# Row sums of the spatial weights: VectorE and a trip through DRAM in place of a TensorE product with ones

## The chip, the cores and the metric

The kernel runs on one core of a Trainium2 chip. TensorE (PE in the profile, PEld for its weight loads) multiplies; VectorE (DVE), ScalarE (ACT) and GpSimd (POOL) compute beside it; SyncE (SP), ScalarE and GpSimd issue DMAs. The metric is the device time of one launch in microseconds (us), compared as a median of runs.

## The reference

Two layers of a bidirectional encoder over 512 positions and 1024 channels, in float32. Each layer normalises its input, projects it into three branches (a gated linear recurrence, a spatial gating unit, windowed attention), gates them, merges them and adds the result to its input. What the change touches is the spatial gating unit:

```python
def layer_norm(x, g, b):
    mu = jnp.mean(xf, axis=-1, keepdims=True)
    var = jnp.mean(jnp.square(xf - mu), axis=-1, keepdims=True)
    return (xf - mu) * lax.rsqrt(var + EPS) * g + b

def spatial_gating(u, v, ln_g, ln_b, w_s, b_s):
    B, L, _ = u.shape
    vn = layer_norm(v, ln_g, ln_b).reshape(B, L // SG_CHUNK, SG_CHUNK, SG_GROUPS, SG_GW)
    mixed = jnp.einsum('gts,bnsgc->bntgc', w_s, vn) + b_s.T[None, None, :, :, None]
    return u * mixed.reshape(B, L, SG_W)
```

There are 4 groups of 128 channels and chunks of 128 positions. The layer norm's bias `b` is the same at every position, so it contributes `b[c]` times the sum over s of `w_s[g, t, s]`. The kernel uses that: it mixes the normalised values without gain and bias, and adds `b[c] * sum_s w_s[g, t, s] + b_s[g, t]` afterwards. These sums, 4 x 128 numbers a layer, are what the change computes in another way.

## The kernel before

Weights come in 512 KB pieces (`wr`, four buffers, loaded through SyncE in a fixed order). Each is split into a high part by ScalarE (L267, `wh`) and a low part by VectorE (L268, `wl`), and TensorE makes three products for each pair of operands. A `t_block` (L517) is 24 such products of 128 x 512, with `main_t` as its caller for the input projection; `nat_part` (L470) does the same in the other orientation. `w_ahead` (L278) issues the split of the next piece, and the loads behind it, at the end of a block.

Around these blocks the smaller work runs as Python generators. After half a block and after its end the main line calls `advance(us)`, which adds that much credit and then steps the first two generators (`WIDTH = 2`) of the list `sides` in turn, each step giving back its cost. A generator that yields `None` is not stepped again in the same call:

```python
        try:
            c = next(g)
        except StopIteration:
            sides.remove(g)
            return 0.0
        if c is None:
            waiting.append(g)
            return 0.0
```

This sets the order of the code. The framework beneath then orders each engine's queue by that order and by when operands are expected to be ready; an instruction wrapped in `pin` stays behind the one before it on its engine. Tiles of one tag share a fixed number of buffers: `t2` (128 x 512 float32) has seven, `small` 24.

The stages around the change, in each layer: projections for attention; values of the recurrence; then, for each of four heads, four blocks, and after two heads the recurrence of that pair joins `sides` (`gla`, with L915 to L974 as its steps up the levels and L992 to L1031 as its end). Attention (`attention`, L783 to L818) is in `sides` from earlier on. At h == 1 the v path of the gating unit is projected (`do_vb`), the generator `ln_v` is put second in `sides`, and, in layer 0, the row of rotary gains and sink logits for the next layer is loaded again (`rope_row`, L336, pinned on SyncE; its one buffer is read by attention up to L792). `do_uz` (L1039 to L1101) projects u and z, with a `t2` tile for z.

`ln_v` takes the statistics of v on VectorE (L1054, L1055), a reciprocal root in small operations (L324 to L331), the sums by a product of `ones` with the transposed spatial weights `ws` (L1059), so that every partition holds all of them, and four operations that turn `br`, the spatial bias on all partitions, into the sum named above (L1062). Then it normalises v in place (L1067). `spatial` (L1073 to L1078) uses `ws`, v and `br` for each group after h == 3.

`ws` and `br` are loaded by `gate_consts` (L352, L354), unpinned, through SyncE. On GpSimd's queue stand attention's two DMAs for each block of probabilities (L817 to DRAM, L818 back), the rotations' (L692, L694), and the saving of parts of the normalised input (L1295).

Of the kernel before, what the change touches and what calls it, by code (L numbers as in the profile page):

```python
# [14 lines left out]
F32 = mybir.dt.float32  # L15
# [3 lines left out]
ALU = mybir.AluOpType  # L19
AX = mybir.AxisListType.X  # L20
PSUM = bass.MemoryType.PSUM

P = 128
# [149 lines left out]
    return bass.AP(a.tensor, a.offset + off, [list(a.ap[0])] + [list(d) for d in dims])  # L173


def hybrid_kernel(tc, x, wpk, brow, gainb, pvec, wsp, trig, amask, imask, out):
    nc = tc.nc
    from contextlib import ExitStack

    with ExitStack() as es:  # L180
        cp = es.enter_context(tc.tile_pool(name="const", bufs=1))
        wp = es.enter_context(tc.tile_pool(name="wts", bufs=4))
        sb = es.enter_context(tc.tile_pool(name="work", bufs=2))
        pp = es.enter_context(tc.tile_pool(name="psum", bufs=3, space=PSUM))
        dp = es.enter_context(tc.tile_pool(name="spill", bufs=1, space=bass.MemoryType.DRAM))
        build(nc, tc, cp, wp, sb, pp, dp, x, wpk, brow, gainb, pvec, wsp, trig, amask, imask, out)


LAG, QLAG = 8, 11
N_M4, N_T2, N_PM, N_PS = 19, 7, 3, 5  # L190


def build(nc, tc, cp, wp, sb, pp, dp, x, wpk, brow, gainb, pvec, wsp, trig, amask, imask, out):
    V, S, G, E = nc.vector, nc.scalar, nc.gpsimd, nc.tensor


# [2 lines left out]
    def nm(s):  # L199
        cnt[0] += 1  # L200
        return f"{s}_{cnt[0]}"
# [7 lines left out]
    def small(n):  # L209
        return sb.tile([P, n], F32, name=nm("sm"), tag="small", bufs=24)  # L210
# [4 lines left out]
    def ps_side(shape=(P, 512), dt=F32):  # L215
        return pp.tile(list(shape), dt, name=nm("ps"), tag="ps", bufs=N_PS)
# [94 lines left out]
    ones = cp.tile([P, P], F32, name="ones")  # L311
# [9 lines left out]
    def rstd(ss, n, scale, order=free, small=small):  # L321

        v, y, a = small(n), small(n), small(n)
        order(V.tensor_scalar(v, ss, -0.5 * scale, -0.5 * EPS, ALU.mult, ALU.add))  # L324

        magic = float(0x5F3759DF - 0x40400000)
        order(V.tensor_scalar(y.bitcast(I32), v.bitcast(I32), -0.5, magic, ALU.mult, ALU.add))
        for _ in range(3):
            order(V.tensor_tensor(a, y, y, ALU.mult))
            order(V.tensor_tensor(a, a, v, ALU.mult))  # L330
            order(V.scalar_tensor_tensor(y, a, 1.5, y, ALU.add, ALU.mult))  # L331
        return y
# [17 lines left out]
    def gate_consts(l, eng):  # L350
        br = cp.tile([P, R_GQ], F32, name=nm("br"), tag="br", bufs=1)
        eng.dma_start(br, brow[l, :R_GQ].partition_broadcast(P))  # L352
        ws = cp.tile([P, 4, P], F32, name=nm("ws"), tag="ws", bufs=1)
        eng.dma_start(ws, wsp[l])  # L354
        return br, ws
# [235 lines left out]
    for l in range(L):  # L591
# [4 lines left out]
        lnb = pvc[:, V_LNB + 4 * l : V_LNB + 4 * l + 4]  # L596
# [57 lines left out]
        def main_t():  # L654
            po = t_block(*w_next(), 0, *hT, KT, lambda: advance(2.6))
            w_ahead(1)
            return po
# [205 lines left out]
        for g in range(4):  # L863
# [6 lines left out]
            po = main_t()  # L870
# [13 lines left out]
        br, ws = gate_consts(l, nc.sync)  # L884
# [162 lines left out]
            gelu(po, vg[tb // 2][:, tb % 2, :])  # L1047

        def ln_v():
            mv = small(8)  # L1050
            mv2 = mv.rearrange("p (n c) -> p n c", c=2)
            for n in range(NT):
                st = small(6)
                V.bn_stats(st, vg[n // 2][:, n % 2, :])  # L1054
                V.bn_aggr(mv2[:, n, :], st)  # L1055
            r = rstd(mv2[:, :, 1], NT, 1.0)

            po = ps_side((P, 4, P))
            E.matmul(po, ones, ws, start=True, stop=True)  # L1059
            for g in range(4):  # L1060
                b = br[:, g * P : (g + 1) * P]
                V.scalar_tensor_tensor(b, po[:, g, :], lnb[:, g : g + 1], b, ALU.mult, ALU.add)  # L1062
            yield 2.5
            yield None
            for n in range(NT):
                v = vg[n // 2][:, n % 2, :]
                V.tensor_scalar(v, v, mv2[:, n, 0:1], r[:, n : n + 1], ALU.subtract, ALU.mult)  # L1067
                yield 0.7

        def spatial(g):  # L1070
            po = ps_side((P, 4, P))
            for n in range(NT):
                E.matmul(po[:, n, :], vg[n // 2][:, n % 2, g * P : (g + 1) * P], ws[:, g, :], start=True, stop=True)  # L1073
            y = t2((P, 4, P))
            bs = br[:, R_BS + g * P : R_BS + (g + 1) * P].unsqueeze(1).broadcast_to((P, 4, P))
            V.scalar_tensor_tensor(y, po, lng[:, g : g + 1], bs, ALU.mult, ALU.add)
            u = uz[g // 2][:, g % 2, :]
            V.tensor_tensor(u, u, y.rearrange("p n t -> p (n t)"), ALU.mult)  # L1078
            yield 2.0
# [15 lines left out]

        glas = []
        lnv, spat = ln_v(), [spatial(g) for g in range(4)]
        for h in range(H):
            po = main_t()
# [4 lines left out]
            for d in range(2):  # L1104
                po = main_t()
                gates(po, d, h, ff, kd)
                advance(2.6)
            po = main_t()
# [272 lines left out]
        def quarter(slot, half):  # L1381
            return three(lambda ts, kt, g: ts[kt][:, slot, 256 * half + g * P : 256 * half + (g + 1) * P], mgh, mgl)
# [57 lines left out]
        def one(terms, handler, *args):  # L1440
            return product(terms, 1, (P, 1, 512), lambda g, po: handler(g, po[:, 0]), *args)

        a = one(quarter(0, 0), p1)
# [15 lines left out]
def host_arrays(inputs):  # L1459
    a = {k: np.asarray(v) for k, v in inputs.items()}  # L1460
    ct = np.ascontiguousarray
    f = a["x"].dtype
    arrays = {}
    arrays["x"] = ct(a["x"].reshape(T, D))
    arrays["wpk"] = pack_weights(a["w_in"], a["w_branch_a"], a["w_branch_b"], a["w_branch_c"], a["w_out"])

    def swap(g):
        return np.concatenate([g[:, 32:], g[:, :32]], axis=1)

    qg, kg = a["q_norm_gain"], a["k_norm_gain"]  # L1470
    arrays["brow"] = ct(
        np.concatenate(
            [
                a["b_spatial"].reshape(L, 512),
                qg,
                swap(qg),
                kg,
                swap(kg),
                a["sink_logits"],
            ],  # L1480
            axis=1,
        )
    )
    arrays["gainb"] = ct(a["norm_gain"])
    lbl = a["lb_logits"].reshape(L, 8, P).transpose(2, 0, 1).reshape(P, 16)
    hgt = a["hg_norm_gain"].transpose(2, 0, 1).reshape(P, 8)
    lnt = [a[n].reshape(L, 4, P).transpose(2, 0, 1).reshape(P, 8) for n in ("sg_ln_gain", "sg_ln_bias")]
    arrays["pvec"] = ct(np.concatenate([lbl, hgt] + lnt, axis=1))
    arrays["wsp"] = ct(a["w_spatial"].transpose(0, 3, 1, 2))

    half = 32
    inv = (10000.0 ** (-np.arange(half, dtype=np.float64) / half)).astype(np.float32)
    ang = np.arange(T, dtype=np.float32)[:, None] * inv[None, :]
    c = np.cos(ang.astype(np.float64)).astype(np.float32)
    s = np.sin(ang.astype(np.float64)).astype(np.float32)
    cc = np.concatenate([c, c], axis=1).reshape(NT, P, 64).transpose(1, 0, 2)
    sn = np.concatenate([-s, s], axis=1).reshape(NT, P, 64).transpose(1, 0, 2)
    arrays["trig"] = ct(np.stack([cc, sn], axis=1))
    qi, ki = np.arange(P)[:, None], np.arange(P)[None, :]
    arrays["amask"] = ct(  # L1500
        np.concatenate(
            [np.where(ki >= qi, 0.0, MASKED), np.zeros((P, P)), np.where(ki <= qi, 0.0, MASKED)], axis=1
        ).astype(np.float32)
    )
    si, ti = (np.arange(P) % 32)[:, None], np.arange(32)[None, :]
    xr = si ^ ti
    masks = [(xr >= m) & (xr < 2 * m) for m in (1, 2, 4, 8)]
    masks += [(xr < 16) & (np.arange(P)[:, None] // 32 == b) for b in range(4)]
    arrays["imask"] = ct(np.stack(masks, axis=1).astype(np.int32))
    assert arrays["x"].dtype == f  # L1510
    return arrays


NAMES = ["x", "wpk", "brow", "gainb", "pvec", "wsp", "trig", "amask", "imask"]


# [16 lines left out]
```

## Time and profile before

| | |
|---|---|
| time, median of 3 runs | 1064.62 us (1064.45 to 1065.05) |
| the profiled execution | 1064.73 us, span 1063.0 us |
| granted TensorE clock | 1.00 |
| TensorE busy | 1054.4 us, 7432 instructions |
| VectorE busy | 799.7 us, 1497 instructions |
| ScalarE busy | 521.4 us, 797 instructions |
| GpSimd busy | 106.7 us, 150 instructions |
| DMA | 162.78 MB, mean 153 GB/s |

The span runs from the first to the last instruction; the profiled execution's own time contains it and what lies around it. A row of a line or a group names the line of the code, the engine and operation, the tile written and those read, and durations in ns (least, median, most). A timeline row gives the start in us, the duration, the engine and the line; "x2" means two instructions merged in one row, and a bracket gives the engine's idle time before it and what ended it. The ends of matmuls are modelled.

### The profile page before, as it was taken

How to read it: one execution, taken by the hardware profiler on the slowest of the kernel's cores; microseconds unless marked ns; L12 is line 12 of the kernel's file. 1: busy time of each engine (PE TensorE's matmuls, PEld its weight loads, DVE VectorE, ACT ScalarE, POOL GpSimd, SP SyncE). 2: the span in 40 equal slices, each digit the busy share in tenths (PEclk: the TensorE clock that was granted, in tenths of full speed). 3: DMA queues.
4: the chain of work that ended last, by engine and by line, in shares of the span. 5: the costliest groups of instructions: out<-in, count | busy, mean ns of one | idle time of the engine just before them, and what ended most of it. 6: DMA issues, size and time to landing. Idle time of an engine off the chain costs nothing.

```text
span 1063.0 us, 18544 instructions
## 1 busy us (share of the span) xinstructions
PE 1054.4 (99%) x7432; PEld 893.7 (84%) x7432; DVE 799.7 (75%) x1497; ACT 521.4 (49%) x797; POOL 106.7 (10%) x150
## 2 busy tenths in 40 slices
PE   8999999999999999999999999999999999999998
PEld 7888877888788998988878888777878889999886
DVE  6884699877877865578887567998678678665885
ACT  5344874464523652545433377656553245345442
POOL 0220111000000100001102201100000001010030
PEclk9999999999999999999999999999999999999999
DMA  8673464252333465665958345543432236466664
GB/s 311 165 226 101 156 199 159 102 183 82 118 120 82 101 195 120 159 221 108 304 162 239 124 137 168 179 133 120 159 107 91 102 60 159 140 142 179 201 174 137
DMA packets 49734, 162.78 MB, mean 153 GB/s; under 512 B 5744, under 2 KB 10352, under 8 KB 49648
## 3 DMA queue, kind: packets, MB, share of 16 engines
q1 hardware_dynamic: 28656, 100.25, 28.6%
q0 software_dynamic: 19264, 57.16, 21.7%
q10 hardware_dynamic: 1728, 4.20, 1.0%
q8 instruction: 58, 0.95, 0.3%
q14 instruction: 28, 0.23, 0.1%
HBM read 139.55 MB, written 22.02 MB: 152 GB/s over the span
## 4 chain that ended last, share of the span: by engine, by line
PE 95%; DVE 2%; DMA 1%; ACT 1%; issue 0%; SPq 0%; ACTq 0%; POOLq 0%; DVEq 0%
PE pm L517 49%; PE pm L470 12%; PE ps L1193 11%; PE pm L1193 11%; PE pm L505 2%; PE ps L831 2%; PE ps L926 1%; PE ps L782 1%; PE ps L781 1%; PE ps L1000 1%; PE ps L1073 1%; PE ps L1012 1%; DMA wr<-in_wpk 1%; PE ps L1016 1%; PE ps L948 1%; DMA hold<-in_wpk 1%
## 5 line engine op out<-in xcount | busy, mean ns | idle before, releaser
L267 ACT CAST wh<-wr 128x1024 fp32r<-128x1024 f32 x160 | 166.7, 1050 | 213.2 <-PE pm L517 135.8
L268 DVE TENSOR_TENSOR wl<-wr,wh 128x1024 fp32r<-128x1024 f32 x160 | 193.5, 1219 | 78.5 <-PE pm L517 32.6
L517 PE MATMUL pm<-hth,wh 128*128 128x512 f32 x576 | 229.9, 399 | 0.0
L517 PE MATMUL pm<-htl,wh 128*128 128x512 f32 x576 | 224.9, 390 | 0.0
L517 PE MATMUL pm<-hth,wl 128*128 128x512 f32 x576 | 224.6, 390 | 0.0
L517 PEld LDWEIGHTS pm<-hth,wh 128*128 128x128 f32 x576 | 108.2, 188 | 25.8 <-issue 2.9
L517 PEld LDWEIGHTS pm<-hth,wl 128*128 128x128 f32 x576 | 108.1, 188 | 22.9
L517 PEld LDWEIGHTS pm<-htl,wh 128*128 128x128 f32 x576 | 108.3, 188 | 20.9 <-issue 0.5
L517 PE MATMUL pm<-m,wh 128*128 128x512 f32 x256 | 89.8, 391 | 0.0
L470 PE MATMUL pm<-wh,hth 128*128 128x512 f32 x192 | 74.4, 397 | 0.7 <-ACT hth L267 0.5
L470 PE MATMUL pm<-wh,htl 128*128 128x512 f32 x192 | 73.5, 392 | 0.2 <-DVE htl L268 0.2
L470 PE MATMUL pm<-wl,hth 128*128 128x512 f32 x192 | 73.2, 391 | 0.0
L972 DVE TENSOR_TENSOR m<-m,f 128x512 f32<-128x512 f32 x96 | 63.2, 685 | 6.3 <-PE ps L948 5.0
L268 DVE TENSOR_TENSOR wl<-hold,wh 128x1024 fp32r<-128x1024 f32 x36 | 43.7, 1221 | 22.6 <-PE pm L1193 16.7
L267 ACT CAST wh<-hold 128x1024 fp32r<-128x1024 f32 x36 | 37.7, 1049 | 43.4 <-PE pm L517 15.6
L517 PEld LDWEIGHTS pm<-m,wh 128*128 128x128 f32 x256 | 47.8, 188 | 9.5
L517 PE MATMUL pm<-t,wl 128*128 128x512 f32 x128 | 50.2, 393 | 0.0
L517 PE MATMUL pm<-t,wh 128*128 128x512 f32 x128 | 50.0, 390 | 0.0
L470 PEld LDWEIGHTS pm<-wh,hth 128*128 128x128 f32 x192 | 36.0, 188 | 10.3 <-issue 1.6
L267 ACT CAST m<-m 128x512 fp32r<-128x512 f32 (+1 forms) x30 | 24.2, 819 | 38.2 <-DVE m L1314 22.1
L470 PEld LDWEIGHTS pm<-wh,htl 128*128 128x128 f32 x192 | 36.0, 188 | 7.7 <-DVE htl L268 0.5
L470 PEld LDWEIGHTS pm<-wl,hth 128*128 128x128 f32 x192 | 36.0, 188 | 7.4
(258 smaller groups left out, 2247.0 us busy)
## 6 DMA issues: line engine op xcount, KB each, us to landing
wr<-in_wpk SPq DMA_DIRECT2D x160, 512.0 KB, 3.9
pd<-m POOLq DMA_DIRECT2D x20, 512.0 KB, 4.0
m<-pd POOLq DMA_DIRECT2D x20, 512.0 KB, 4.8
hold<-in_wpk POOLq DMA_DIRECT2D x18, 512.0 KB, 5.5
hold<-in_wpk SPq DMA_DIRECT2D x12, 512.0 KB, 4.9
wr<-in_wpk POOLq DMA_DIRECT2D x12, 512.0 KB, 7.0
m<-in_x SPq DMA_DIRECT2D x8, 512.0 KB, 6.7
m<-xd POOLq DMA_DIRECT2D x16, 256.0 KB, 6.9
```

The source lines that it names most:

```text
L267: order(S.copy(hi_dst, src))
L268: order(eng.tensor_tensor(lo_dst, src, hi_dst.bitcast(F32), ALU.subtract))
L470: E.matmul(po, a, b[:, o : o + 512], start=first and n == 0, stop=last and n == len(passes) - 1)
L505: E.matmul(po[:, k, :], a, b[:, o : o + 256], start=n == 0, stop=n == 23)
L517: E.matmul(po, s, m, start=n == 0, stop=n == 3 * nk - 1)
L781: E.matmul(sp[:, :nk], qt[qb][:, h, :], ktt[0][:, g, k0 * P : k1 * P], start=True, stop=False)
L782: E.matmul(sp[:, :nk], qt[qb][:, h, :], ktt[1][:, g, k0 * P : k1 * P], start=False, stop=True)
L831: E.matmul(po[64 * g : 64 * g + 64], vC[:, k0 + kb, 64 * g : 64 * g + 64], pt[:, :, 128 * g : 128 * g + 128], start=kb == 0, stop=kb == le ...
L926: E.matmul(cb[p0 : p0 + 32, slot, j // 4, :], kk(32 * j), qq(32 * j), start=True, stop=True, tile_position=(0, p0),)
L948: E.matmul(dg[p0 : p0 + 32, j // 4, f0 : f0 + 32], kx[:, 32 * j : 32 * j + 32] if m == 16 else k_op(32 * j, m), q_op(32 * jq, m), start=Tr ...
L972: V.tensor_tensor(v, v, custom(ff, of, ([sd, 2], [2, ng], [0, m])), ALU.mult)
L1193: E.matmul(banks[g][:, r, :], a, b, start=not onto and (r, kt, n) == (0, 0, 0), stop=kt == 3 and n == 2, skip_group_check=onto is not None ...
```

## The change

The host hands over the spatial weights in a second layout, `wsr`, with the position t on the partitions and s innermost. `ln_v` begins with a `t2` tile `wsum`, which is loaded with them through SyncE, and then yields `None` three times. After that VectorE sums over s, which leaves one number for each t (partition) and group. GpSimd's queue writes these 128 x 4 numbers to DRAM in the order group, t, and reads them back, to every partition, into the same `wsum`. The product with ones is gone; the four operations on `br` read `wsum` in place of PSUM, and stand after the normalisation of v in place of before it. Two yields of 0.5 are added.

```diff
+    arrays["wsr"] = ct(a["w_spatial"].transpose(0, 2, 1, 3))
...
         def ln_v():
+
+            wsum = t2((P, 4, P))
+            nc.sync.dma_start(wsum, wsr[l])
+            for _ in range(3):
+                yield None
+            ss = small(4)
+            V.tensor_reduce(ss, wsum, AX, ALU.add)
+            sd = dp.tile([4, P], F32, name=nm("sd"))
+            G.dma_start(sd.rearrange("g t -> t g"), ss)
+            G.dma_start(wsum.rearrange("p g t -> p (g t)"), sd.rearrange("g t -> (g t)").partition_broadcast(P))
+            yield 0.5
             mv = small(8)
             mv2 = mv.rearrange("p (n c) -> p n c", c=2)
             for n in range(NT):
@@
                 V.bn_aggr(mv2[:, n, :], st)
             r = rstd(mv2[:, :, 1], NT, 1.0)
-
-            po = ps_side((P, 4, P))
-            E.matmul(po, ones, ws, start=True, stop=True)
-            for g in range(4):
-                b = br[:, g * P : (g + 1) * P]
-                V.scalar_tensor_tensor(b, po[:, g, :], lnb[:, g : g + 1], b, ALU.mult, ALU.add)
             yield 2.5
             yield None
             for n in range(NT):
                 v = vg[n // 2][:, n % 2, :]
                 V.tensor_scalar(v, v, mv2[:, n, 0:1], r[:, n : n + 1], ALU.subtract, ALU.mult)
                 yield 0.7
+
+            for g in range(4):
+                b = br[:, g * P : (g + 1) * P]
+                V.scalar_tensor_tensor(b, wsum[:, g, :], lnb[:, g : g + 1], b, ALU.mult, ALU.add)
+            yield 0.5
```

More of the change, by code (lines that the diff above doesn't have):

```diff
@@ L173, in custom, with hybrid_kernel @@
     return bass.AP(a.tensor, a.offset + off, [list(a.ap[0])] + [list(d) for d in dims])
-def hybrid_kernel(tc, x, wpk, brow, gainb, pvec, wsp, trig, amask, imask, out):
+def hybrid_kernel(tc, x, wpk, brow, gainb, pvec, wsp, wsr, trig, amask, imask, out):
     nc = tc.nc
@@ L185, in hybrid_kernel, with build @@
         dp = es.enter_context(tc.tile_pool(name="spill", bufs=1, space=bass.MemoryType.DRAM))
-        build(nc, tc, cp, wp, sb, pp, dp, x, wpk, brow, gainb, pvec, wsp, trig, amask, imask, out)
+        build(nc, tc, cp, wp, sb, pp, dp, x, wpk, brow, gainb, pvec, wsp, wsr, trig, amask, imask, out)
 LAG, QLAG = 8, 11
 N_M4, N_T2, N_PM, N_PS = 19, 7, 3, 5
-def build(nc, tc, cp, wp, sb, pp, dp, x, wpk, brow, gainb, pvec, wsp, trig, amask, imask, out):
+def build(nc, tc, cp, wp, sb, pp, dp, x, wpk, brow, gainb, pvec, wsp, wsr, trig, amask, imask, out):
     V, S, G, E = nc.vector, nc.scalar, nc.gpsimd, nc.tensor
@@ L1511, in host_arrays @@
     return arrays
-NAMES = ["x", "wpk", "brow", "gainb", "pvec", "wsp", "trig", "amask", "imask"]
+NAMES = ["x", "wpk", "brow", "gainb", "pvec", "wsp", "wsr", "trig", "amask", "imask"]
 def kernel(**inputs):
```

## The prediction

> **What bounds the kernel now.** I read the page's busy times and its chain first, then the timeline around the product with ones, then the windows and queues around the same places.
>
> ```profile
> PE 1054.4 (99%) x7432; PEld 893.7 (84%) x7432; DVE 799.7 (75%) x1497; ACT 521.4 (49%) x797; POOL 106.7 (10%) x150
> PE 95%; DVE 2%; DMA 1%; ACT 1%; issue 0%; SPq 0%; ACTq 0%; POOLq 0%; DVEq 0%
> ...
> PEld ps L831 <- issue: 4.2, 14, 0.4
> PEld pm L517 <- ACT m L1039: 0.8, 1, 0.8
> ```
>
> The page gives the engines' busy time, then the shares of the chain that ended last. TensorE holds 95% of that chain, so whatever leaves its queue shortens the kernel, as long as nothing new makes it wait. The last two rows are waits of weight loads from 130 to 300 us (total, times, longest), the costliest of all and the costliest on another engine: 0.8 us there; TensorE is fed in time.
>
> The product with ones (L1059) is two instructions in each layer. The ends are modelled with overlap, so I take its cost from start to start:
>
> ```profile
> 180.55 0.39 PE L517 MATMUL pm<-htl,wh 128*128 128x512 f32 x1
> 180.78 0.40 PE L517 MATMUL pm<-hth,wl 128*128 128x512 f32 x1
> 181.01 1.02 PE L1059 MATMUL ps<-ws,ones 128*128 128x512 f32 x2
> 181.47 0.80 PE L517 MATMUL pm<-hth,wh 128*128 128x512 f32 x1
> 182.10 0.39 PE L517 MATMUL pm<-htl,wh 128*128 128x512 f32 x1
> ...
> 703.47 0.40 PE L517 MATMUL pm<-hth,wl 128*128 128x512 f32 x1
> ...
> 704.80 0.39 PE L517 MATMUL pm<-htl,wh 128*128 128x512 f32 x1
> ```
>
> Neighbours start 0.23 us apart. From 180.78 to 182.10 pass 1.32 us with one ordinary product between; without the ones it would be 2 x 0.228 = 0.46. The ones cost 0.86 us in layer 0, and by 703.47 to 704.80 (1.33 us) 0.87 in layer 1: 1.73 us together.
>
> **The change part by part.**
>
> *TensorE: the product goes.* Minus 1.73 us, on the chain. Bounds: the modelled duration of the pair in both layers, 2 x 1.02 = 2.04, above; 0 below, if TensorE then waits for what the ones covered. I take 1.73, since the rows next to it show no wait.
>
> *VectorE: one sum and four moved operations a layer.*
>
> ```profile
> L1020 DVE TENSOR_REDUCE sm<-t x8: 675/678/687, 241.1 to 879.9; 128x4 f32<-128x512 f32 x8
> L1062 DVE SCALAR_TENSOR_TENSOR br<-ps,pvc,br x8: 318/339/348, 182.6 to 706.4; 128x128 f32<-128x128 f32 x8
> 175.00:200.00 25.00, 25.00 (x234) 20.48 (x220) 24.27 (x69) 9.22 (x14) 0.77 (x1) 1.00 0.24 85
> 697.00:722.00 25.00, 25.00 (x238) 20.26 (x237) 24.27 (x72) 13.34 (x24) 0.75 (x1) 1.00 0.41 143
> ```
>
> L1020 is a reduction of the new one's exact shape: 2 x 0.678 = 1.36 us more. L1062's eight remain with SBUF as source; no row has that operand, so 0.339 again, between half of it and as much more. The windows give the stretch, its length, then busy time and count of PE, PEld, DVE, ACT and POOL, the clock, the DMA share and GB/s: VectorE is busy 24.27 of 25 us just here. So the extra work isn't covered by idle time of VectorE. It is covered by what in that queue may run later: the recurrence steps (L941, L972) and attention. I cost it at nothing, with 1.36 as the other end if TensorE follows VectorE there.
>
> *SyncE: a load of 256 KB a layer.* The nearest load is that of ws:
>
> ```profile
> L354 SPq DMA_DIRECT2D ws<-in_wsp x2: 327/328/328, 17.0 to 321.3; - x2
> ws<-in_wsp SPq DMA_DIRECT2D x2, 256.0 KB, 4.2
> 203.55 0.33 SPq L336 DMA_DIRECT2D rr<-in_brow  x1
> SPq L336 <- DVE sm L792: 27.2, 1, 27.2
> L436 DVE TENSOR_TENSOR sm<-pvc x1: 160/160/160, 74.1 to 74.1; 128x8 f32<-128x8 f32 x1
> ```
>
> It costs 0.33 us of the queue and lands after 4.2. In layer 0 it meets the queue at rest: from 176.4 SyncE waits 27.2 us for attention's last use of sink (L792) before it reloads rr at 203.55, with the weight loads pinned behind. ws shows that an unpinned load goes as soon as its buffer is free: 17.0 us, though the code has it after do_ia. For a shared pool the order of the code seems to hold: L436 needs only pvc and a small buffer, yet starts at 74.1, where the code has it. So I place the load at the first step of ln_v, past the waiting rr, near 177 us. Cost nothing. Were it behind rr, the sums would come some 27 us later, and I bound that by L1076 below, which needs them only at 294.
>
> The buffer is one of seven t2, held from there to the end of ln_v (some 15 to 25 us). The recurrence pair stands still in that time, and TensorE's only claim on t2 is the z of do_uz. I cost it at nothing; if a z had to wait, its PSUM bank would too.
>
> *GpSimd: two DMAs a layer, the first in 4-byte pieces.*
>
> ```profile
> q0 software_dynamic: 19264, 57.16, 21.7%
> t<-vd POOLq DMA_DIRECT2D x8, 64.0 KB, 2.6
> br<-in_brow SPq DMA_DIRECT2D x2, 256.0 KB, 4.9
> L1295 POOL DMA_DIRECT2D h<-hth x2: 768/838/907, 30.5 to 553.2; - x2
> 220.72 0.56 POOL L817 DMA_DIRECT2D pd<-m  x1 [44.32 <-DVE m L813]
> 745.78 0.56 POOL L817 DMA_DIRECT2D pd<-m  x1 [44.11 <-DVE m L813]
> ```
>
> No row has 4-byte pieces. Below: t<-vd, 128 pieces of 512 bytes in 2.6 us. Above: a packet of queue q0 (packets, MB, share of 16 engines' span) holds an engine 0.217 x 16 x 1063 / 19264 = 0.19 us. By that t<-vd's 8 pieces an engine are 1.5 of its 2.6 us, which leaves 1.1 for start and finish; the new write's 32 an engine are 6.1, with the 1.1 together 7.2. I take the middle, 4.9, since its pieces are far smaller than any of q0's. The second DMA is br's shape, one row of 2 KB to all partitions: 4.9. It waits for the first, and queued behind it is nothing: POOL rests 44 us before its next issue at 220.72 and at 745.78. An issue takes 0.56 to 0.91.
>
> [...]
>
> *The new wait: four operations behind a DMA.* Chain: reduction 0.68, issue 0.56, write 4.9, issue 0.56, broadcast 4.9: 11.6 us (long end 0.68 + 0.91 + 7.2 + 0.91 + 6.8 = 16.5; 6.8 is br's longest, in the first row below). The four then stand at the end of ln_v's VectorE work, which covers it:
>
> ```profile
> DMA to landing us min/median/max: 3.1/4.9/6.8
> 177.66 0.69 DVE L1054 BATCH_NORM_STATS2 sm<-m 128x6 f32<-128x512 f32 x1
> 191.83 0.54 DVE L1067 TENSOR_SCALAR m<-m,sm,sm 128x512 f32<-128x512 f32 x1
> 700.35 0.69 DVE L1054 BATCH_NORM_STATS2 sm<-m 128x6 f32<-128x512 f32 x1
> 712.02 1.92 DVE L1067 TENSOR_SCALAR m<-m,sm,sm 128x512 f32<-128x512 f32 x4
> L1076 DVE SCALAR_TENSOR_TENSOR t<-ps,pvc,br x8: 744/746/753, 294.1 to 838.7; 128x512 f32<-128x512 f32 x8
> ```
>
> From the first statistics to the last normalisation it is 14.7 us (177.66 to 192.37) and 13.6 (700.35 to 713.94), against 11.6: no wait. The reader of the sums, L1076, comes 100 us later, so only the place in VectorE's queue can hurt: behind a waiting L1062 stand the weight split (L268) and the PSUM readers that TensorE needs.
>
> *The order.* ln_v now sits out three rounds of `advance` before its work and asks 1.0 more of credit. As second of the two active generators it keeps the recurrence pair out for up to three rounds, 7.8 us of side work, while attention has the turns alone. Attention's last use of sink comes no later for that, so rr and the weights behind it don't either. What a new order costs TensorE I bound by the layers, which do the same products in different orders:
>
> ```profile
> 74.53 21.76 PE pm L470 x96
> 498.63 2.72 PE ps L1193 x12
> 597.23 21.76 PE pm L470 x96
> 1020.78 2.72 PE ps L1193 x12
> ```
>
> 74.53 to 498.63 is 424.10 us, 597.23 to 1020.78 is 423.55: 0.55 apart. I take 0 and allow 0.55 either way for the two layers.
>
> **Sum.** -1.73 + 0 + 0 + 0 + 0 = -1.73 us. The profiled execution took 1064.73 us (span 1063.0), 0.11 above the median of 1064.62: 1063.0 in its terms, 1062.9 as median. A measurement of this kernel tells about 0.2%, 2.1 us, from no change: the forecast lies inside, between 1062.5 and 1066.7.
>
> **Rivals.**
> 1. *The order falls better as well.* The gaps before products of small tiles (L831 above: 14 of them, 4.2 us, 0.3 each) could grow fewer, three over both layers. For it: attention runs more by itself. Against: L831's come in every batch. 1.73 + 0.9 gives 1062.0.
> 2. *VectorE hands its extra work on.* It is full in both windows, and all 1.36 us reach TensorE: 1064.62 - 1.73 + 1.36 = 1064.3. Against: no wait on VectorE of any size shows.
> 3. *Slower: VectorE stands at the first L1062 until the broadcast has landed.* At the long end the shortfalls are 16.5 - 14.7 = 1.8 and 16.5 - 13.6 = 2.9, 4.7 us; if TensorE pays all, 1064.62 - 1.73 + 4.7 = 1067.6. It decides from 3.8 us on TensorE (1.73 + 2.1), so the chain must be near 16 us in both layers. For it: a full VectorE has no slack to give back. Against: L268 is issued a block of products (24 x 0.23 = 5.4 us) ahead. [...] With 2 KB to move I give that 1 in 100. [...]
> 4. *The change doesn't act where it is put.* Both loads go out at the start, as ws did at 17.0, and hold two of seven t2 for long. 512 KB more in a start that moves 311 GB/s cost 1.7 us if all of it delays the first weights, and eat the gain: 1064.6. L436 speaks against it.
>
> ```profile
> GB/s 311 165 226 101 156 199 159 102 183 82 118 120 82 101 195 120 159 221 108 304 162 239 124 137 168 179 133 120 159 107 91 102 60 159 140 142 179 201 174 137
> ```
>
> **How the numbers follow.** Forecast, 1062.3 to 1063.4: 0.42, of which 0.08 lies below 1062.5. Rival 1, down to 1061.5: 0.17. Rival 2 and smaller waits, 1063.4 to 1066.7: 0.26. Rival 3: 0.12 with its extreme. Rival 4: 0.03. Faster 0.17 + 0.08 = 0.25; slower 0.12; same the other 0.63. The range 1061.5 to 1065.8 leaves out rival 3 and the edges.
>
> **What would show it.** No product at L1059's place, and neighbours 0.23 us apart there. The wsum load from SyncE near 177 us, ahead of rr. A reduction of 0.68 us, POOL's write landing in 2.6 to 7.2 us, the broadcast after it. The four operations starting right after VectorE's previous one: idle time before them, put down to a DMA, is rival 3. TensorE's waits on VectorE still in tenths. The forecast is wrong if the reordering moves a layer by more than 0.55 us, or if a z waits for a t2 buffer.

## The result, and the profile after

The changed kernel takes 1076.01 us (median of 4, 1075.74 to 1077.15) against 1064.57 for the kernel before beside it: ratio 1.0109 [1.0091, 1.0126], 11.4 us slower. The forecast was 1062.9, the range ended at 1065.8, and "slower" had 0.12.

Lines have moved: the load of the second layout is L1052, the reduction L1056, the write to DRAM L1058, the read-back L1059, the statistics L1065, the normalisation L1072. The four operations on `br`, L1062 before, are now L1077. First the page of the kernel after: busy times, granted clock by slice, shares of the chain that ended last.

```profile
PE 1055.9 (98%) x7428; PEld 894.1 (83%) x7428; DVE 800.6 (75%) x1499; ACT 518.2 (48%) x795; POOL 109.7 (10%) x154
PEclk9999999989999999999999999998999999999999
PE 85%; issue 5%; DVE 4%; DMA 4%; ACT 1%; POOL 0%; SPq 0%; POOLq 0%; DVEq 0%; ACTq 0%
```

TensorE has four instructions fewer, and its share of the chain fell from 95% to 85%. DMA, VectorE and "issue" took what it lost. The clock has an 8 in two slices that had none. All of it lies in one place in each layer. The next rows are from the waits (total, times, longest):

```profile
DVE br L1077 <- DMA t<-sd: 11.5, 2, 6.0
PE ps L948 <- DVE m L972: 10.2, 2, 5.4
POOL t L1059 <- DMA sd<-sm: 18.2, 2, 9.8
```

VectorE stood 11.5 us at the first L1077 until the sums came back, and TensorE 10.2 us at a product of the recurrence (L948) that needed VectorE's L972. In the kernel before, the waits of TensorE show none at that step. The sequence in layer 0 is in the timelines of VectorE, POOL and TensorE (start, duration, and in brackets the idle time before with its releaser):

```profile
198.53 0.68 DVE L1065 BATCH_NORM_STATS2 sm<-m 128x6 f32<-128x512 f32 x1
198.91 0.86 POOL L1058 DMA_DIRECT2D sd<-sm  x1 [22.80 <-DVE sm L1056]
207.04 0.15 DVE L329 TENSOR_TENSOR sm<-sm 128x4 f32<-128x4 f32 x1
208.19 0.55 POOL L1059 DMA_DIRECT2D t<-sd  x1 [8.41 <-DMA sd<-sm]
212.64 0.35 DVE L1077 SCALAR_TENSOR_TENSOR br<-t,pvc,br 128x128 f32<-128x128 f32 x1 [5.44 <-DMA t<-sd]
213.57 1.98 DVE L1072 TENSOR_SCALAR m<-m,sm,sm 128x512 f32<-128x512 f32 x4
213.88 0.39 PE L517 MATMUL pm<-htl,wh 128*128 128x512 f32 x1
218.26 0.68 DVE L972 TENSOR_TENSOR m<-m,f 128x512 f32<-128x512 f32 x1
219.08 0.65 PE L948 MATMUL ps<-m,t 128*32 128x32 f32 x32 [4.81 <-DVE m L972]
```

From the write's issue to the read-back's it is 9.28 us here and, by the same rows of layer 1, 10.52. VectorE reached the first L1077 at 207.2, ahead of the normalisation, not behind it as in the code. TensorE's last product before its wait began at 213.88.

In each of the two waits the granted clock falls from 1.00 to 0.50, and it stays there behind the wait, to 223.07 and 752.14 us. The windows below give start and end, length, busy time and count of PE, PEld, DVE, ACT, POOL, then the clock, the DMA share and GB/s:

```profile
216.00:218.00 2.00, 0.00 (x0) 0.00 (x0) 2.00 (x4) 0.24 (x1) 0.54 (x1) 0.56 0.86 229
218.00:220.00 2.00, 0.92 (x33) 0.83 (x33) 1.94 (x5) 0.00 (x0) 0.00 (x0) 0.50 0.72 295
220.00:222.00 2.00, 2.00 (x37) 0.94 (x38) 2.00 (x5) 0.00 (x0) 0.76 (x1) 0.50 0.03 8
222.00:224.00 2.00, 2.00 (x10) 0.64 (x8) 1.64 (x3) 0.00 (x0) 0.00 (x0) 0.73 0.80 221
```

Busy time times the missing share of the clock is 0.92 x 0.5 + 2 x 0.5 + 2 x 0.27 = 2.0 us; the same windows of layer 1 (747 to 753) give 1.36 x 0.5 + 2 x 0.5 + 2 x 0.28 = 2.2. So the price is 10.2 us of waiting and 4.2 us lost to half speed behind it, 14.4 in all.

### The profile page after: what moved, and what is told of

Its sections match the earlier page's. It is cut to its first block, busy times and chain, and to the rows that moved or that the text cites. A ratio compares the mean times of both kernels' runs of the same rounds, so it can differ in the third digit from the quotient of the medians.

```text
span 1074.2 us, 18554 instructions
## 1 busy us (share of the span) xinstructions
PE 1055.9 (98%) x7428; PEld 894.1 (83%) x7428; DVE 800.6 (75%) x1499; ACT 518.2 (48%) x795; POOL 109.7 (10%) x154
## 3 DMA queue, kind: packets, MB, share of 16 engines
q0 software_dynamic: 19488, 57.68, 21.6%
## 4 chain that ended last, share of the span: by engine, by line
PE 85%; issue 5%; DVE 4%; DMA 4%; ACT 1%; POOL 0%; SPq 0%; POOLq 0%; DVEq 0%; ACTq 0%
PE pm L517 43%; PE ps L1203 11%; PE pm L1203 11%; PE pm L470 9%; PE pm L505 2%; DMA sd<-sm 2%; PE ps L831 1%; PE ps L1000 1%; PE ps L926 1%; DMA t<-sd 1%; PE ps L782 1%; PE ps L781 1%; PE ps L1012 1%; PE ps L1083 1%; PE ps L948 1%
## 5 line engine op out<-in xcount | busy, mean ns | idle before, releaser
L268 DVE TENSOR_TENSOR wl<-wr,wh 128x1024 fp32r<-128x1024 f32 x160 | 193.1, 1218 | 74.4 <-PE pm L517 42.0
L972 DVE TENSOR_TENSOR m<-m,f 128x512 f32<-128x512 f32 x96 | 63.2, 682 | 4.5 <-PE ps L948 2.4
L268 DVE TENSOR_TENSOR wl<-hold,wh 128x1024 fp32r<-128x1024 f32 x36 | 43.8, 1221 | 23.6 <-PE pm L1203 15.3
L262 POOL DMA_DIRECT2D hold<-in_wpk x18 | 15.6, 868 | 314.8 <-DVE wl L268 313.6
```

The lines of the kernel that those rows point to most:

```text
L262: G.dma_start(r, wpk[add], accum_op=ALU.add)
L268: order(eng.tensor_tensor(lo_dst, src, hi_dst.bitcast(F32), ALU.subtract))
L972: V.tensor_tensor(v, v, custom(ff, of, ([sd, 2], [2, ng], [0, m])), ALU.mult)
```

## The experiments

**Is it the wait at L1077?** Theory A: VectorE stands at L1077 for the DMA chain, and TensorE behind it. Theory B: the other order of the work is dear. Theory C: VectorE's added work or the `t2` buffer is.

*Consumers held behind the normalisation:*

```
-                V.scalar_tensor_tensor(b, wsum[:, g, :], ...)
+                pin(V.scalar_tensor_tensor(b, wsum[:, g, :], ...))
```

> The four operations that read the sums stand behind the normalisation (L1072) in VectorE's queue, TensorE's and ScalarE's queues being the same as in the changed kernel. Theory A, that VectorE stands at L1077 until the broadcast has landed and TensorE waits behind it at L948: VectorE has 4.1 us more to do first (L813 1.2, L1101 0.65, L941 0.3, four L1072 1.98), its two waits of 5.4 and 6.0 us shrink to 1.3 and 1.9, TensorE gets back 8.2 us and some of the time at a low clock: 1066 to 1068. Theory B, that the new order of the side work costs the time by itself: 1076. Theory C, that VectorE's extra sum or the t2 buffer held costs it: 1076.

1063.92 us, ratio 0.9993 [0.9984, 1.0002]. The same write, TensorE's and ScalarE's queues in the same order, and 12.1 us of the loss are gone. VectorE still waits, but less (its timeline, both layers), and so does TensorE (its waits):

```profile
212.54 1.14 DVE L1077 SCALAR_TENSOR_TENSOR br<-t,pvc,br 128x128 f32<-128x128 f32 x4 [1.09 <-DMA t<-sd]
735.20 1.14 DVE L1077 SCALAR_TENSOR_TENSOR br<-t,pvc,br 128x128 f32<-128x128 f32 x4 [1.93 <-DMA t<-sd]
PE ps L948 <- ACT m L893: 1.5, 1, 1.5
PE ps L948 <- DVE m L972: 0.4, 1, 0.4
```

So the place of four operations in VectorE's queue makes most of the loss. The time is under what theory A was given, because only 1.9 us of TensorE's time were lost and the clock stayed at 1.00 in every window behind them.

*A write of 128 rows of 16 bytes:*

```
-            sd = dp.tile([4, P], F32, name=nm("sd"))
-            G.dma_start(sd.rearrange("g t -> t g"), ss)
+            sd = dp.tile([P, 4], F32, name=nm("sd"))
+            G.dma_start(sd, ss)
```

> The write to DRAM keeps the order t, group, in 128 pieces of 16 bytes in place of 512 of 4; the sums then sit in wrong places. TensorE's queue is that of the changed kernel. Theory A: the write of 8.75 to 10.0 us shrinks to about a quarter of its part over 1.1, near 3.1, the broadcast lands before VectorE asks for it, no wait at L1077 nor at L948: 1062.9 plus what the order costs, 1062.5 to 1064.5. Theory B: 1076. Theory C: 1076.

1061.87 us, ratio 0.9973 [0.9963, 0.9984], under the expected 1062.5. The queues of TensorE, VectorE and ScalarE hold the same instructions in the same order as after. From the timeline of POOL, issue to issue:

```profile
198.96 0.68 POOL L1058 DMA_DIRECT2D sd<-sm  x1 [22.82 <-DVE sm L1056]
201.31 0.57 POOL L1059 DMA_DIRECT2D t<-sd  x1 [1.67 <-DMA sd<-sm]
```

2.35 us in place of 9.28 (3.04 in layer 1), the sums arrive before VectorE asks, and nothing waits. The 14.1 us between the two kernels are the write's layout alone.

*The kernel before with the change's rounds and nothing else:* three `yield None` ahead of `ln_v`'s work and the two added yields of 0.5.

> The kernel before, product with ones kept, with only the three empty rounds at the head of ln_v and the two yields of 0.5. Theory A: no wait on a DMA, 1064.6 within 1. Theory B: 1076 plus the 1.7 of the product, 1077.7. Theory C: 1064.6.

1064.47 us, ratio 0.9999 [0.999, 1.0008]. The statistics moved from 177.66 to 198.31, as in the kernel after (198.53), and it cost nothing: theory B falls.

*Read-back and consumers far behind the write.* The read-back goes into a `t2` tile of its own after h == 3, and the consumers stand six rounds behind it:

```
-            G.dma_start(wsum.rearrange(...), sd.rearrange("g t -> (g t)").partition_broadcast(P))
+            sds.append(sd)
```

> All of the change, but the read-back from DRAM goes into a t2 buffer of its own at h == 3 and the four operations come six rounds later; the first buffer is free after the sum. Theory A: nothing stands behind the chain, 1062.9, between 1062 and 1064. Theory B: 1076. Theory C: as far as the buffer is to blame 1063, as far as the sum is 1076.

1062.44 us, ratio 0.9979 [0.997, 0.9988]. The 4-byte write and the reduction remain, and the loss is gone. The first `t2` tile is free after the sum here; in the run with 16-byte rows it is held as in the kernel after, and the loss is gone there as well. So theory C falls too.

**How the loss grows.** *Pieces of 8 bytes:*

```
-            sd = dp.tile([4, P], F32, name=nm("sd"))
-            G.dma_start(sd.rearrange("g t -> t g"), ss)
+            sd = dp.tile([2, P, 2], F32, name=nm("sd"))
+            G.dma_start(sd.rearrange("a t b -> t a b"), ss.rearrange("t (a b) -> t a b", b=2))
```

> The kernel after, with one size changed: the sums leave in 256 pieces of 8 bytes in place of 512 of 4 bytes (and come back in that order, so two of the four groups' sums stand at wrong places). The orders of TensorE, VectorE and ScalarE are those of after. Theory A (the time is the wait at L1077 for the DMA chain, and TensorE's idle time behind it with the low granted clock that follows): the write takes between the 2.3 to 3.0 us of 16-byte pieces and the 8.75 to 10.0 us of 4-byte pieces, about 4.5 to 5.5, so the first L1077 waits 1 to 2.5 us a layer in place of 5.4 and 6.0, TensorE waits at L948 for 0.3 to 1.9 us a layer, too short for the low clock (the granted clock stays above 0.95 between 218 and 230 us), and the time is 1063 to 1066. Rival D (the loss goes with the wait, low clock included, in proportion): 14.1 us of loss for 10.2 us of TensorE idle, so 1.4 us for each us of wait; 1063 to 1067 and a clock somewhat down. Rival E (the cost is in POOL's transposing write as such, not in its length): near 1076.

1061.77 us, ratio 0.9974 [0.9965, 0.9983], under the expected 1063: no wait at all, since the write takes 3.81 us in layer 0 and 4.46 in layer 1 (issue to issue, the first below), less than expected. That waits of up to 1.9 us are too short for the low clock was the author's estimate; none came here.

```profile
198.94 0.71 POOL L1058 DMA_DIRECT2D sd<-sm  x1 [22.77 <-DVE sm L1056]
202.75 0.58 POOL L1059 DMA_DIRECT2D t<-sd  x1 [3.09 <-DMA sd<-sm]
```

*A second write of 4-byte pieces ahead of the real one:*

```
+            sd0 = dp.tile([4, P], F32, name=nm("sd")); G.dma_start(sd0.rearrange("g t -> t g"), ss)
             sd = dp.tile([4, P], F32, name=nm("sd"))
```

> The kernel after, with a second, unread write of the same 512 pieces of 4 bytes put ahead of the real one on POOL's queue; the orders of TensorE, VectorE, ScalarE and SyncE are those of after. Theory A: if the two writes' pieces go one after the other, the real sums land some 8 to 10 us a layer later; the first L1077 waits 13 to 16 us, TensorE at L948 as much less 0.6, and the low clock's price stays what it is in after (about 2 us a layer) since the clock is already at half: 1076.0 + 2 x 9 = 1094, between 1090 and 1098. Rival D (loss in proportion, 1.4 for each us of wait): 1101. Rival F (the writes of 4-byte pieces run beside each other, so that length is latency and not throughput): 1076 to 1079.

1078.05 us, ratio 1.0126 [1.0112, 1.014]: rival F. Twice the pieces delay the landing by only about 1 us a layer (199.04 to 209.11 from first issue to read-back in POOL's timeline, 10.07 against 9.28, and 11.54 against 10.52 in layer 1). TensorE's waits rise from 10.2 to 11.6 and the span from 1074.2 to 1075.8. The dose turned out too small to separate theory A from D.

*VectorE held by arithmetic in place of the wait.* Two kernels with the 16-byte rows, in which a long reduction stands ahead of the first consumer (9 or 13 times 512 elements):

```
+                if g == 0: V.tensor_reduce(small(4), wsum.unsqueeze(2).broadcast_to((P, 4, 9, P)), XY, ALU.add)
```

> The kernel with 16-byte rows and strided consumers (1061.8), in which VectorE, in place of a wait, works: one reduction over the broadcast sums, 9 times 512 elements (0.63 us for 512 in the change's own reduction, so about 5.2 us), stands ahead of the first consumer. VectorE's, ScalarE's, POOL's and SyncE's order is else the same; TensorE has four projection products (4 x 0.39 us) moved ahead of the recurrence product L948. No DMA is waited for. The lateness of VectorE is 5.2 us, of which 0.6 (as in after) and 1.6 are covered: TensorE waits at L948 for 2.6 to 3.4 us a layer. [...] If the clock falls at this idle time too: 2 us a layer more, 1071 to 1073. If the delay of VectorE isn't what TensorE pays for: 1061.8 to 1063.

> The same with 13 times 512 elements, about 7.5 us, and the same order: TensorE waits 4.8 to 5.6 us a layer at L948, as long as in the kernel after, and no DMA is waited for. Theory A (the low clock comes of TensorE's idle time, whatever caused it): 1061.8 + 2 x 5.2 + 4 = 1076, between 1074.5 and 1077.5, with a granted clock near 0.5 over some 4 us behind each wait. If the low clock belonged to the DMA traffic and not to the idle time: 1071 to 1073, and no such stretch.

1073.18 us, ratio 1.0077 [1.0064, 1.0091], and 1078.58, ratio 1.0125 [1.0111, 1.0138], with 1065.11 for the kernel before on that chip. No DMA is waited for, and 13 times 512 elements cost about as much as the change (1.0109). So TensorE pays for VectorE's lateness, whatever VectorE is late for. The shorter one had the low clock too, which its expectation left open, and lies 0.2 us above the 1071 to 1073 given for that case. The longer one lies 1.1 us above its range, and most of its wait, 7.1 of 9.0 us, stands at a projection product behind L1102 in place of L948. These are TensorE's waits of the shorter one that VectorE or ScalarE caused around L948, then its windows in layer 0:

```profile
PE pm L517 <- DVE t L1102: 2.9, 2, 1.4
PE ps L948 <- DVE m L972: 1.8, 3, 0.8
PE pm L517 <- ACT m L890: 1.4, 2, 0.7
216.00:220.00 4.00, 1.46 (x60) 0.93 (x62) 4.00 (x8) 0.57 (x1) 0.54 (x1) 0.99 0.32 131
220.00:222.00 2.00, 2.00 (x34) 0.74 (x21) 2.00 (x5) 0.00 (x0) 0.76 (x1) 0.50 0.03 8
222.00:224.00 2.00, 2.00 (x10) 0.61 (x6) 1.38 (x3) 0.00 (x0) 0.00 (x0) 0.66 0.89 258
```

6.1 us of waiting in pieces of at most 1.45 us, and yet the clock is at half from 220 us on, 1.7 us of work in this layer. No single idle time was long; TensorE was busy 1.46 of 4 us. In finer windows the clock changes only at the edges of steps that are 3.41 us long: the falls of the two layers, at 219.95 and 745.60 us, lie 154 such steps apart (of 3.413 us), and the five changes of the kernel after, at 216.25, 223.07, 745.31, 752.14 and, behind the last product, 1072.99, lie 2, 153, 2 and 94 apart. These windows of the same run are cut along them:

```profile
213.12:216.54 3.42, 2.20 (x9) 1.19 (x7) 3.42 (x8) 2.37 (x4) 0.00 (x0) 1.00 0.01 5
216.54:219.95 3.41, 1.37 (x55) 0.88 (x59) 3.41 (x8) 0.03 (x1) 0.54 (x1) 1.00 0.37 154
219.95:223.36 3.41, 3.41 (x40) 1.27 (x32) 3.41 (x7) 0.00 (x0) 0.76 (x1) 0.50 0.40 97
223.36:226.78 3.42, 3.42 (x77) 2.10 (x74) 2.16 (x7) 0.00 (x0) 0.00 (x0) 1.00 0.67 219
```

TensorE was busy for 1.37 us of the second step, and the third runs at half speed; after the first, with 2.20 us busy, the clock had stayed. The kernel after spends two steps at half speed in each layer, 216.25 to 223.07 and 745.31 to 752.14 us. So the clock fell without an idle step: here after 1.37 us of work in the step, and in layer 0 of the kernel after only 2.0 us behind the last product's modelled end (214.27), after a step with 1.44 us of work.

Against the 16-byte kernel, by their ratios to before, the two cost 10.9 and 16.0 us. Waits and missing clock, both layers, explain 6.1 + 3.3 and 9.0 + 6.1; 1.5 and 0.9 us stay unexplained. TensorE's order differs in them: four projection products stand earlier.

**What the write costs, and what the product does.** *The 4-byte write alone*, issued behind a real write of 16-byte rows and followed by a read of one element, which goes out when the write has landed:

```
+            if l == 0: sa = dp.tile([4, P, 16], F32, ...); G.dma_start(sa[:, :, 0].rearrange("g t -> t g"), ss)
+            else:      sa = dp.tile([4, P], F32, ...);     G.dma_start(sa.rearrange("g t -> t g"), ss)
+            G.dma_start(small(4)[0:1, 0:1], sa[...])
```

> A measurement of the 4-byte write alone, beside the kernel with 16-byte rows and strided consumers: behind the real write the sums leave once more in 512 pieces of 4 bytes, in layer 0 each into 64 bytes of its own, in layer 1 side by side as in the change; one element of it is read back on POOL's queue, whose issue shows when the write had landed (and may hold POOL's later transfers up: the time of the whole is not the question). Theory G (pieces side by side in one stretch of memory hold each other up): layer 0 about 3 to 5 us from the write's issue to the read's, layer 1 9 to 11.5. Theory H (it is the number of pieces): both 9 to 11.5.

From POOL's timeline, layer 0 (64 bytes apart), then layer 1 (side by side):

```profile
199.73 0.76 POOL L1062 DMA_DIRECT2D sa<-sm  x1
204.67 0.55 POOL L1063 DMA_DIRECT2D sm<-sa  x1 [2.70 <-DMA sa<-sm]
721.44 0.76 POOL L1066 DMA_DIRECT2D sa<-sm  x1
730.14 0.55 POOL L1067 DMA_DIRECT2D sm<-sa  x1 [5.78 <-DMA sa<-sm]
```

4.94 against 8.70 us with 512 pieces both times, one instance in each layer; 8.70 is a little under the expected 9 to 11.5. The layers' own difference in the kernel after is 1.24 us, a third of these 3.76. So lying side by side costs 2.5 to 3.8 us, and the number of pieces (4.94 against 2.35 for the rows) some 2.6. No run here shows by what mechanism.

*The whole computation with the layout mended:* 16-byte rows, and the consumers read the sums with a stride of four.

```
-                V.scalar_tensor_tensor(b, wsum[:, g, :], ...)
+                V.scalar_tensor_tensor(b, wsum.rearrange("p g t -> p (g t)").rearrange("p (t g) -> p g t", g=4)[:, g, :], ...)
```

> The whole computation, with the layout mended: the sums leave as 128 rows of 16 bytes, come back as they stand (each partition holds t by g), and the four consumers at L1077 read them with a stride of 4 elements. The orders of the engines are those of after. Theory A: as the run with 16-byte rows, the chain lands before VectorE asks (no wait at L1077 over 0.3 us, none at L948), each L1077 costs up to 0.2 us more for its stride, off the path: 1061.5 to 1062.6, ratio 0.997 to 0.998. A rival, that the strided read is slow (each L1077 over 0.8 us in place of 0.35) and VectorE's 4 x 0.45 us reach the path as the wait at L948 would: 1063 to 1065.

1061.81 us, ratio 0.9975 [0.9966, 0.9985]: 2.7 us under the kernel before and 14 under the kernel after: the version that beats both. The stride costs 0.43 us a consumer in place of 0.35, off the path.

*The same with the product kept, unread:*

```
+            po = ps_side((P, 4, P))
+            E.matmul(po, ones, ws, start=True, stop=True)
```

> The kernel with 16-byte rows and strided consumers, and beside it the product with ones kept at its old place in ln_v after the statistics, with no reader. It prices the product by itself, against that kernel in the same call. Theory A's step (TensorE's 0.86 and 0.87 us, start to start): 1.7 us over that kernel, 1063.4 to 1064.3. A rival, that the gain of 2.7 us with 16-byte rows came from elsewhere than the product (the order of the queues, the earlier waits of weight loads): 0 to 0.8 us over that kernel, 1061.7 to 1062.6.

1063.88 us, ratio 0.9993 [0.9984, 1.0001]. The product costs 2.07 us (1063.88 - 1061.81), with whatever the order of the queues adds, which differs a little from the kernel without it. The other 0.67 of the 2.74 us gained is not placed by any run; the order alone gave 0.1 (1064.59 to 1064.47).

*A version with more cover:* load, sums and write (16-byte rows) a stage earlier (the write goes out at 83.7 us in place of 198.9, 115 us early and not the expected 60), the read-back into a buffer of its own after the fourth head, consumers six rounds later.

> The whole computation, as a version that has cover on all sides: load, sums and their write (16-byte rows) begin with the block ahead of the projections, some 60 us early, the read-back goes into a buffer of its own after the fourth head, the strided consumers stand six rounds behind it, and ln_v keeps no round of its own for them. Theory A: no wait at the consumers, none for TensorE; 2.07 us for the product gone and the rest by the order of the queues: 1061.4 to 1062.8. A rival, that the two t2 buffers and the earlier loads hold SyncE up and weight loads come late: 1063 to 1065.

1068.99 us, ratio 1.0035 [1.0021, 1.0049]: the expectation was wrong by 7 us. The waits name the cause, again the change's own:

```profile
DVE br L1087 <- DMA t<-sd: 3.0, 2, 1.6
PE ps L941 <- DVE pc L951: 3.2, 2, 1.7
POOL t L1082 <- PE ps L831: 61.2, 2, 31.3
272.00:274.00 2.00, 0.86 (x65) 0.65 (x64) 0.41 (x2) 1.25 (x2) 0.00 (x0) 1.00 1.00 363
274.00:276.00 2.00, 1.47 (x58) 0.97 (x62) 2.00 (x7) 0.00 (x0) 0.00 (x0) 0.78 0.62 248
276.00:278.00 2.00, 2.00 (x28) 1.65 (x20) 2.00 (x5) 0.00 (x0) 0.00 (x0) 0.50 0.05 12
```

POOL held the read-back until an attention product of TensorE (L831) was done, so it went out shortly before its readers; L1087, the consumer here, stood for it, the copy L951 behind it was late, and TensorE waited for that. A wait of 1.7 us was followed by a clock of 0.50 in layer 0. Waits and clock make 4.9 us (3.2 + 1.7). Against the version with strided consumers the span is 6.7 longer, of which 0.55 is the chip (before took 1065.11 there, 1064.55 on the other); the remaining 1.2 stays open. The spread of its five runs goes with the clock: the mean granted clock was 1.000 in the run of 1066.35 us, 0.998 in those of 1068.37 and 1068.99, and 0.997 in those of 1070.00 and 1070.03, which is what none, one and two steps at half speed would leave, at some 1.7 us each.

## Why the prediction was wrong

- *TensorE, -1.73:* right in direction, a little small. The unread product costs 2.07; the outer bound was 2.04.
- *VectorE's reduction, the load, the `t2` buffer, at 0:* held. The version with 16-byte rows has the same three in place and is faster than before. The load went out at 162.9 us, not 177, after SyncE had stood 11 us in each layer for a free `t2` buffer (from the waits), a wait that the prediction did not have and that cost that version nothing which shows:

```profile
SPq L1052 <- PE ps L926: 22.1, 2, 11.1
```

- *The order, 0 within 0.55:* held (0.9999).
- *POOL's write, 4.9 with 7.2 as its upper bound:* failed. It took 8.75 and 10.0 us by the chain of waits, against 4.4 and 3.8 for the broadcast, which came in under its 4.9:

```profile
198.91 8.75 DMA sd<-sm
208.19 4.42 DMA t<-sd
726.87 10.00 DMA sd<-sm
737.39 3.77 DMA t<-sd
```

  The bound scaled a time per packet of larger pieces, one packet for each piece. But in the kernel after that queue has only 224 packets more (19488 against 19264), for both layers' writes and read-backs together, and from 204 to 208 us and 732 to 736 us, with the write still on its way, the DMA share is 0.00. So by this record the time is not the engines' work on packets, and no other transfer held the write up then. Between 128, 256 and 512 pieces the time from issue to issue went 2.35, 3.81, 9.28: the last doubling is out of line with a price per piece, and the padded write shows part of why. The prediction also had nothing queued behind it on POOL. But the statistics came later than in the kernel before, and attention's L817 went out straight after the read-back, at 208.73 us. With held consumers it stood there too (208.89), at little cost.
- *"The new wait", the step that decided.* It took the whole of `ln_v` as cover, 14.7 and 13.6 us, since the code has the four operations last. The framework put the first three ahead of the normalisation, and the stretch from the write's issue to the first L1077 was 8.3 us (198.91 to 207.2). A chain of 14 us against that leaves 5.4. Even the forecast's own 11.6, less the reduction's 0.68, would have been 2.6 too long.
- *Rival 3 was the mechanism,* and mis-priced at 1067.6. It took the long end of the chain but kept the cover of 14 us; it saw TensorE's risk in the weight split (L268), where the tie was the recurrence step; and it had no term for the clock, 4.2 us. The extreme in its chance, the 1 in 100, stands on no run: the slowest single write here took 10.52 us from issue to issue, two at once 11.54.
- The sum by measured terms: 1064.57 - 2.07 - 0.67 (not placed) + 10.2 + 4.2 = 1076.2, against 1076.01.

## What to carry to other kernels

Cover for a DMA is counted from its issue to the place of its first reader in the engine's queue as scheduled, not in the source; where the order is a scheduler's, a reader that needs a DMA must be held back or given its data a stage early. A tiny transfer is laid out by what the writer has contiguous, and the reader takes the stride: 0.08 us an operation here against 7 us of DMA. When TensorE's idle time is priced, the clock behind it is priced too: here 4.2 us behind 10.2 us of wait, and in steps, about 1.7 us of lost work for each 3.41 us at half speed.

## What the runs showed of the hardware

- 2 KB from 128 partitions to DRAM: 2.35 us in 16-byte rows, 3.81 in 8-byte, 9.28 in 4-byte pieces side by side, 4.94 in 4-byte pieces 64 bytes apart (issue to issue, layer 0). Two 4-byte writes, issued 0.75 us apart, took 0.79 us longer than one in layer 0 (10.07 against 9.28) and 1.02 in layer 1 (11.54 against 10.52).
- The granted clock went to 0.50 in steps of 3.41 us: two in each layer of the kernel after, of the one with two writes and of the longer held one, one in each layer of the shorter held one (219.95 to 223.36 and 745.60 to 749.02), one in layer 0 of the last version. It did so not only after gaps near 5 us but after 2.8 to 3.3 us of idle time in pieces of at most 1.45 (the shorter held one), and once after 1.66 us among small products (the last version).
- From full speed, the step ran at 0.50 behind steps with TensorE busy for 0.32 and 1.44 us (kernel after), 1.31 and 1.37 (the shorter held one) and some 1.75 (last version, layer 0). It stayed at 1.00 behind steps with 1.87 us (last version, layer 1), 2.18 (kernel after, 8.04 to 11.46 us) and 2.20 (the shorter held one). So a wait of 1.46 us with held consumers, which leaves at least 1.95 busy in any such step, and of 1.54 in layer 1 of the last version left the clock at 1.00. From half speed it came back behind steps with 3.18 us busy (the shorter held one, layer 1) and 3.41 (kernel after), not behind 0.58 and 1.09 (kernel after) or some 2.8 (the longer held one, layer 0). Busy time rests on modelled ends of products, so these figures are estimates, and so few steps set no bound.
